# One decoder layer with GLA and DeltaNet heads on one core: the instruction order from the scheduler's timeline model in place of its default order

## The chip, the cores and the metric

The kernel runs on one core of one Trainium2 chip, as one program. The metric is the device time of one execution in microseconds; the kernel before takes 2975.47 us (median of three runs, 2974.47 to 2977.1).

## The reference, cut to what matters

One layer is computed for 512 prompt frames and 64 sample frames together, D = 2048, everything in float32:

```
mod = silu(c) @ w_ada + b_ada                   # 6 vectors of 2048, from 2048 x 12288 weights
h   = rmsnorm(x, norm1) * (1 + sc1) + sh1
proj = h @ w_in                                 # 2048 x 7200: 8 GDN heads, 4 GLA heads, gates
o_a = GLA(q, k, v, gate)                        # blocked causal recurrences
o_b = gated DeltaNet(conv(q), conv(k), conv(v)) # with a triangular solve per block
x  += g1 * (concat(o_a, o_b) @ w_out)
h   = rmsnorm(x, norm2) * (1 + sc2) + sh2
x  += g2 * (conv_ffn(h, w_up, w_down))          # 5632 wide, gate branch with a causal conv
y   = rmsnorm(x, final_norm)
```

The outputs are y for both streams and the new recurrent and convolution states.

## The kernel before, in words

The work is laid out with features on the 128 partitions and 576 frames on the free axis (two halves of 288). Each product is made in float32r parts: a weight tile of 128x1024 is loaded (`raw`), rounded by ACT into `wh` (L595) and DVE subtracts the rest, `wl` (L596); `mm6` (L508, L510) then issues three products (high by high, high by low, low by high), two matmuls each. This text calls these weight matmuls, and those of L774, L678, L679, L674 in the head and L1261 to L1263 in the FFN, gemm matmuls; the program has 18816 of them. A gemm tile of the input projection (`in_tile`) is 16 blocks of 128 rows of weights, 96 gemm matmuls.

The stages follow each other:

- The head (`head`): the first two blocks of the modulation are made on TensorE from `w_ada` (L674, and L678 and L679 with split weights), x is normalised and transposed, and the first two projection tiles run with it.
- The heads (`gdn_heads`, then `gla_heads`): for each of eight GDN heads four gemm tiles (q, k, v, gate), each followed by a convolution on ACT and DVE (`gdn_conv`, L880 to L891); then four GLA heads. Beside the gemms run *jobs*: Python generators (`gdn`, `gla`) that make the recurrence of a head, whose steps are emitted one per `tick`, after every mm6. A GDN job transposes k and q on PE (L140 in `transpose4`), makes decay tiles on ACT (`m<-m,ncum`, `m<-m,cum`, exponentials, `m<-m,nbeta`), solves a triangular system (`inverse16`: GpSimd for blocks of 16, with a trip through DRAM and L358 on DVE at its end, then levels L234, L240, L140, L249, L254 of PE and DVE in turn), and then goes through four blocks of 128 frames: L272 on PE, a correction on DVE (`sq`), L279 on PE, a copy on ACT (`sq`), L285 on PE, the new state on DVE (`st`), with L299 and L301 for the output, which ACT scales by `rq`. The rest ends with squares on ACT, L133 on DVE and L134 on GpSimd (an inverse root), four scalings `m<-m,s` and a transpose (L140). What a job issues on DVE and ACT goes through `_Sooner`, which lists it 80 places earlier in priority, and its record line is L1583.
- Also ticked: the rest of the modulation (`ada_blocks`, 16 blocks) is accumulated on DVE, from 512-KB loads of `w_ada` (`xr`): L736 first, then L738, two for each 128 rows of weights, and eight small matmuls (L744) at the end of a block.
- The output projection `w_out` with residual, then the FFN: 44 steps of seven products (`up_product`, L1261 to L1263), then `down`, then the final norm.

The buffers that the heads share are in `_MixPool`: 14 tiles `m`, 6 `qkv`, 3 `gt`. PSUM has two tiles `g` for gemm tiles and four `bank`s.

What sets the order: the kernel's Python code emits instructions in one sequence, with priorities (`high_priority`, offsets AHEAD and JOB_AHEAD), rests (`rest`, REST_T, REST_D, REST_X, REST_N: a job sits out so many steps) and rates (JOB_RATE, ADA_RATE). The tile layer's scheduler then lays this out as one in-order queue for each engine (PE, ACT, DVE, GpSimd as POOL, and SyncE as SP, which issues the DMAs), with semaphore waits where an instruction needs another engine's result. `TileContext` (L1641) is where the scheduler is chosen.

## Time and profile before

| | |
|---|---|
| median of three runs | 2975.47 us (2974.47 to 2977.1) |
| the profiled execution, its own time | 2976.19 us |
| span in its trace | 2974.5 us |
| TensorE's mean granted clock | 0.988 |
| busy: PE, DVE, ACT, POOL | 97%, 70%, 42%, 11% |
| read from and written to DRAM over the span | 131 GB/s |

One execution is recorded, and the times of the rows come from it. A window row gives the span of the window, then for PE, weight loads (PEld), DVE, ACT and POOL the busy time and in brackets the number of instructions, then the granted clock of TensorE as a share of full speed, the busy share of the DMA engines and GB/s. A row of waits gives the waiting engine and line, who released it, the total in us, how many times, and the longest. A group's row gives line, engine, operation, output and input tiles with their shapes and the count, then busy time in us, mean ns of one, then the idle time ahead of these instructions and what ended it. A timeline row gives start, duration, engine and line. float32 matmuls of the jobs run as two passes, each an entry of its own in the trace. L1583 stands for whatever a job issues on DVE and ACT.

### The profile page before, as it was taken

Reading aid. Unit: us, or ns where it says so; the run is one execution under the profiler, and the core shown is the slowest. Engines: PE = TensorE matmul, PEld = TensorE weight load, DVE = VectorE, ACT = ScalarE, POOL = GpSimd, SP = SyncE. Lnnn points to the kernel's source line nnn. Section 1 sums busy time; section 2 is a strip of 40 time slices with the busy share of each in tenths; the row PEclk is TensorE's granted clock in tenths of the full one; section 3 lists DMA queues with packets and bytes.
Section 4 is the critical chain, followed back from the end, with each engine's and each line's share of the span. In section 5 each row is a group of like instructions: output and inputs, shape, how many; then the busy total and the mean of one; then the engine's idle time right before and its main releaser. Section 6 shows DMA issues by size and latency. Waiting matters only on the chain.

```text
span 2974.5 us, 52619 instructions
## 1 busy us (share of the span) xinstructions
PE 2888.2 (97%) x21128; PEld 2786.8 (94%) x21128; DVE 2090.4 (70%) x3226; ACT 1238.0 (42%) x2116; POOL 340.5 (11%) x610
## 2 busy tenths in 40 slices
PE   7988999999999999999999999999999999999998
PEld 3588899999999998999999999999999999999997
DVE  5775667776578777357888888888888865555555
ACT  6555544544343333245444444444444431222223
POOL 0032333332200000000111111111101100000000
PEclk8999999999999999999999999999999999999999
DMA  7854545554444455543334333333333473333221
GB/s 270 290 143 135 148 125 148 146 149 139 138 141 142 137 164 160 158 142 94 105 105 116 105 105 109 112 98 106 115 105 105 135 235 102 111 102 116 83 83 66
DMA packets 532601, 392.96 MB, mean 132 GB/s; under 512 B 58729, under 2 KB 463204, under 8 KB 532356
## 3 DMA queue, kind: packets, MB, share of 16 engines
q1 hardware_dynamic: 532356, 389.59, 43.8%
q8 instruction: 167, 2.74, 0.4%
q14 instruction: 78, 0.64, 0.1%
HBM read 355.16 MB, written 34.36 MB: 131 GB/s over the span
## 4 chain that ended last, share of the span: by engine, by line
PE 65%; DVE 1%; DMA 1%; ACT 0%; issue 0%; POOL 0%; SPq 0%; ACTq 0%; POOLq 0%; DVEq 0%
PE g L508 20%; PE bank L1262 11%; PE bank L1261 11%; PE bank L1263 11%; PE g L510 10%; PE bank L401 1%; DVE acc L738 0%; PE bank L140 0%; DMA xr<-in_x_prompt_dram 0%; PE bank L744 0%; PE bank L1471 0%; POOL s L134 0%; DVE m L1583 0%; DMA raw<-in_w_out_dram 0%; DMA sd_ak<-ts 0%
## 5 line engine op out<-in xcount | busy, mean ns | idle before, releaser
L1262 PE MATMUL bank<-slot,wh 128*128 128x290 f32 x2464 | 736.7, 299 | 0.0
L1261 PE MATMUL bank<-slot,wh 128*128 128x290 f32 x2464 | 735.5, 298 | 0.0
L1263 PE MATMUL bank<-slot,wl 128*128 128x290 f32 x2464 | 728.0, 295 | 0.0
L508 PE MATMUL g<-slot,wh 128*128 128x288 f32 x3168 | 551.6, 295 | 0.2 <-DVE slot L1031 0.2
L595 ACT ACTIVATE wh<-raw 128x1024 fp32r<-128x1024 f32 x223 | 235.4, 1058 | 608.6 <-PE g L508 582.1
L1263 PEld LDWEIGHTS bank<-slot,wl 128*128 128x128 f32 x2464 | 471.8, 191 | 0.0
L1262 PEld LDWEIGHTS bank<-slot,wh 128*128 128x128 f32 x2464 | 469.5, 191 | 0.1
L508 PEld LDWEIGHTS g<-slot,wh 128*128 128x128 f32 x3168 | 465.1, 188 | 0.7 <-DVE slot L1031 0.5
L1261 PEld LDWEIGHTS bank<-slot,wh 128*128 128x128 f32 x2464 | 463.9, 188 | 0.1
L508 PE MATMUL g<-hh,wh 128*128 128x288 f32 x1984 | 453.1, 307 | 1.4 <-DVE cb L881 1.0
L510 PE MATMUL g<-hh,wl 128*128 128x288 f32 x1984 | 443.2, 302 | 3.2 <-DVE wl L596 3.2
L508 PE MATMUL g<-hl,wh 128*128 128x288 f32 x1984 | 439.8, 301 | 0.0
L1031 DVE SCALAR_TENSOR_TENSOR slot<-g,mod,slot 128x512 f32<-128x512 f32 (+1 forms) x448 | 201.8, 491 | 310.4 <-PE g L510 304.1
L738 DVE SCALAR_TENSOR_TENSOR acc<-xr,ct,acc 128x512 f32<-128x512 f32 x480 | 339.5, 753 | 37.0 <-DMA xr<-in_w_ada_dram 36.7
L510 PE MATMUL g<-slot,wl 128*128 128x288 f32 x1584 | 343.0, 295 | 0.0
L510 PEld LDWEIGHTS g<-hh,wl 128*128 128x128 f32 x1984 | 324.4, 191 | 4.2 <-DVE wl L596 3.7
L508 PEld LDWEIGHTS g<-hh,wh 128*128 128x128 f32 x1984 | 323.6, 191 | 4.9 <-DVE cb L881 1.2
L508 PEld LDWEIGHTS g<-hl,wh 128*128 128x128 f32 x1984 | 324.3, 191 | 1.1 <-issue 0.7
L596 DVE TENSOR_TENSOR wl<-raw,wh 128x1024 fp32r<-128x1024 f32 x223 | 272.2, 1222 | 55.2 <-ACT wh L595 54.5
L1208 ACT ACTIVATE wh<-raw 128x1024 fp32r<-128x1024 f32 x176 | 186.0, 1057 | 223.5 <-PE bank L1262 190.3
L510 PEld LDWEIGHTS g<-slot,wl 128*128 128x128 f32 x1584 | 255.1, 188 | 0.0
L1209 DVE TENSOR_TENSOR wl<-raw,wh 128x1024 fp32r<-128x1024 f32 x176 | 215.4, 1224 | 54.1 <-ACT wh L1208 54.1
(361 smaller groups left out, 3418.1 us busy)
## 6 DMA issues: line engine op xcount, KB each, us to landing
raw<-in_w_up_dram SPq DMA_DIRECT2D x176, 512.0 KB
xr<-in_w_ada_dram SPq DMA_DIRECT2D x128, 512.0 KB
raw<-in_w_in_dram SPq DMA_DIRECT2D x108, 512.0 KB
raw<-in_w_down_dram SPq DMA_DIRECT2D x88, 512.0 KB
hraw<-in_w_ada_dram SPq DMA_DIRECT2D x64, 512.0 KB
raw<-in_w_out_dram SPq DMA_DIRECT2D x32, 512.0 KB
slot<-actd SPq DMA_DIRECT2D x44, 288.0 KB
actd<-v SPq DMA_DIRECT2D x44, 256.0 KB
```

The source lines that it names most:

```text
L401: T.matmul(ps[:, b * 64:(b + 1) * 64], e3[:, b], qc[:, b * 64:(b + 1) * 64], start=True, stop=True)
L508: T.matmul(ps[:, h if bank is None else bank, :n], wh, x[:, h, :n], start=f, stop=False)
L510: T.matmul(ps[:, h if bank is None else bank, :n], wl, ah[:, h, :n], start=False, stop=stop)
L595: nc.scalar.activation(hi[:, :n_], raw[:, :n_], AF.Copy)
L596: nc.vector.tensor_tensor(lo[:, :n_], raw[:, :n_], hi[:, :n_].bitcast(F32), op=ALU.subtract)
L738: V.scalar_tensor_tensor(acc[s], w[:, k], col, acc[s], op0=ALU.mult, op1=ALU.add)
L1031: self.nc.vector.scalar_tensor_tensor(x1[:, :, z], ps[:, :, c], gain[:, q:q + 1], x1[:, :, z], op0=ALU.mult, op1=ALU.add)
L1208: self.nc.scalar.activation(hi, src, AF.Copy)
L1209: self.nc.vector.tensor_tensor(lo, src, hi.bitcast(F32), op=ALU.subtract)
L1261: T.matmul(ps, wh[:, j], hi, start=(c < 3 and j == 0), stop=False, skip_group_check=True)
L1262: T.matmul(ps, wh[:, j], lo, start=False, stop=False, skip_group_check=True)
L1263: T.matmul(ps, wl[:, j], hi, start=False, stop=(j == NPAIR - 1), skip_group_check=True)
```

## The change

One argument: the tile layer's scheduler is asked to place the instructions by a simulated timeline of the engines, in place of its default order.

```diff
-    with tile.TileContext(nc) as tc:
+    with tile.TileContext(nc, schedule_with_timeline_sim=True) as tc:
         layer_kernel(tc, i, o)
```

The instructions of both programs are the same, except that ACT loads its function tables five times more. What moves is the order on each engine, and with it the waits. The gemm matmuls keep their order among themselves in the heads. The steps of the GDN jobs stand later relative to them: counted in gemm matmuls on PE ahead of the same instruction, by 26 at the first (557 before, 583 now), 168 where 889 were, 837 where 1636 were, 875 where 2389 were; then the difference shrinks to 85 at 3659 and to about 30 at 5400. Some gemm tiles end with a stretch of job matmuls alone: 23 at gemm matmul 2496, 29 at 2880, 28 at 3264, 83 at 3552, 21 at 3648 and 80 at 3744; before, the longest in the heads is 20. SP issues the first loads of `w_in` 5 to 10 places earlier among those of `w_ada`. In the FFN the first two matmuls of the third and of the fifth of a step's products now stand ahead of the last 22 and 24 of the product before them.

Three places. The first is PE in an early GDN job, where a step of the inverse goes from L240 (`bank_420`) over DVE to the transpose L140 (`bank_421`). Before:

```order
L240 MATMUL bank_420_2279<-m_344_1674,m_384_2033 128x64 x4
L508 MATMUL g_471_2544<-hh_227_1048,wh_473_2546 128x288
L508 MATMUL g_471_2544<-hl_228_1049,wh_473_2546 128x288 x2
L510 MATMUL g_471_2544<-hh_227_1048,wl_474_2547 128x288 x2
L508 MATMUL g_471_2544<-hh_230_1071,wh_473_2546 128x288 x2
L508 MATMUL g_471_2544<-hl_231_1072,wh_473_2546 128x288
L140 MATMUL bank_421_2292<-consts0_91,m_385_2034 128x128 x4
L234 MATMUL bank_430_2329<-m_385_2034,m_359_1774 128x64 x4
```

Now, the last twelve rows ahead of and with the same transpose; its L240 stands seven rows above this piece:

```order
L508 MATMUL g_508_2895<-hh_167_828,wh_510_2897 128x288 x2
L508 MATMUL g_508_2895<-hl_168_829,wh_510_2897 128x288 x2
L510 MATMUL g_508_2895<-hh_167_828,wl_511_2898 128x288 x2
L508 MATMUL g_508_2895<-hh_170_851,wh_510_2897 128x288 x2
L508 MATMUL g_508_2895<-hl_171_852,wh_510_2897 128x288 x2
L510 MATMUL g_508_2895<-hh_170_851,wl_511_2898 128x288 x2
L508 MATMUL g_508_2895<-hh_227_1048,wh_510_2897 128x288 x2
L508 MATMUL g_508_2895<-hl_228_1049,wh_510_2897 128x288 x2
L510 MATMUL g_508_2895<-hh_227_1048,wl_511_2898 128x288 x2
L508 MATMUL g_508_2895<-hh_230_1071,wh_510_2897 128x288 x2
L508 MATMUL g_508_2895<-hl_231_1072,wh_510_2897 128x288
L140 MATMUL bank_421_2292<-consts0_91,m_385_2034 128x128 x4
```

Eight gemm matmuls stood between the two, and now 32 do.

The second is PE and ACT at the end of a GDN job, at gemm matmul 2880: from the last outputs (`bank_815`, `bank_822`, scaled by ACT into `m_791`) to the transpose of the normalised output (`bank_827`). PE before:

```order
L299 MATMUL bank_822_4990<-sq_819_4977,m_631_3736 128x128
L301 MATMUL bank_822_4990<-st_814_4952,qkv_605_3549 128x128
L510 MATMUL g_785_4828<-hh_322_1494,wl_812_4940 128x288 x2
L508 MATMUL g_830_5048<-hh_161_782,wh_832_5050 128x288 x2
L508 MATMUL g_830_5048<-hl_162_783,wh_832_5050 128x288 x2
L510 MATMUL g_830_5048<-hh_161_782,wl_833_5051 128x288 x2
L508 MATMUL g_830_5048<-hh_164_805,wh_832_5050 128x288 x2
L508 MATMUL g_830_5048<-hl_165_806,wh_832_5050 128x288 x2
```

PE now:

```order
L301 MATMUL bank_815_4954<-st_803_4908,qkv_605_3549 128x128
L272 MATMUL bank_816_4964<-st_814_4952,m_655_3930 128x128
L279 MATMUL bank_818_4975<-sq_817_4965,m_732_4427 128x128
L285 MATMUL bank_820_4986<-sq_819_4977,m_636_3768 128x128
L299 MATMUL bank_822_4990<-sq_819_4977,m_631_3736 128x128
L301 MATMUL bank_822_4990<-st_814_4952,qkv_605_3549 128x128
L140 MATMUL bank_827_5030<-consts0_91,m_791_4857 128x128
L744 MATMUL bank_850_5277<-consts0_91,acc_738_4530 128x1
```

The gemm matmuls of tile `g_830` followed the L301 of `bank_822`; now the transpose `bank_827` follows it at once. ACT there, before:

```order
L1583 ACTIVATE sq_825_5003,s8_823_5001<-m_791_4857 128x128
L595 ACTIVATE wh_845_5217<-raw_844_5216 128x1024
L1583 ACTIVATE m_791_4857<-bank_822_4990,rq_638_3780 128x128
L1583 ACTIVATE sq_825_5003,s8_823_5001<-m_791_4857 128x128
L930 ACTIVATE gt_828_5043<-g_785_4828 128x512
L1583 ACTIVATE sq_825_5003,s8_823_5001<-m_791_4857 128x128
L931 ACTIVATE ts_829_5045<-g_785_4828 128x64
L1583 ACTIVATE sq_825_5003,s8_823_5001<-m_791_4857 128x128
L1583 ACTIVATE m_791_4857<-m_791_4857,s8_824_5002 128x128 x4
```

ACT now, the last twelve rows of the same stretch; four scalings by ncum, an `sq`, a square, four scalings by cum and a table load stand between the scaling of `bank_815` and these rows:

```order
L1583 ACTIVATE m_867_5392<-m_867_5392 128x512
L1583 ACTIVATE sq_825_5003,s8_823_5001<-m_791_4857 128x128
L1583 ACTIVATE m_791_4857<-bank_822_4990,rq_638_3780 128x128
L890 ACT_TABLE_LOAD
L890 ACTIVATE qkv_975_6184<-ca_977_6186 128x512
L1583 ACT_TABLE_LOAD
L1583 ACTIVATE m_868_5393<-m_868_5393 128x512
L1583 ACTIVATE m_866_5390<-m_866_5390 128x512
L1583 ACTIVATE sq_825_5003,s8_823_5001<-m_791_4857 128x128
L1583 ACTIVATE m_867_5392<-m_867_5392,nbeta_1609 128x128 x4
L886 ACTIVATE ca_1018_6464<-cb_1017_6463,cols_172 128x579
L1583 ACTIVATE sq_825_5003,s8_823_5001<-m_791_4857 128x128
```

Between the scaling of `bank_815` and the four scalings `m_791<-m_791,s8_824`, which come next now, the opening of the next head's job (tiles `m_866` to `m_868`, with `L890` and `L886` of a convolution and three table loads) has moved in.

The third is DVE at gemm matmul 3552, in the next job's inverse: from the masking of `bank_1112` to that of `bank_1116` (`m_984`), with the update of `m_1087` between. Before:

```order
L1583 TENSOR_TENSOR m_984_6216<-bank_1112_7108,consts384_1530 128x256
L133 TENSOR_SCALAR s8_1105_7063<-s8_1104_7062 128x4
L738 SCALAR_TENSOR_TENSOR acc_1069_6756<-xr_1143_7326,ct_186,acc_1069_6756 128x512
L738 SCALAR_TENSOR_TENSOR acc_1070_6757<-xr_1143_7326,ct_186,acc_1070_6757 128x512
L1583 TENSOR_TENSOR m_1087_6911<-m_1087_6911,bank_1113_7121 128x16x16
L133 TENSOR_SCALAR rq_1110_7089<-s8_1109_7088 128x4
L1583 TENSOR_SCALAR rq_1110_7089<-rq_1110_7089 128x4
L1583 TENSOR_TENSOR m_984_6216<-bank_1116_7148,consts384_1530 128x256
L1583 TENSOR_TENSOR m_1087_6911<-m_1087_6911,bank_1117_7161 128x8x32
L1583 COPY m_984_6216<-bank_1122_7192 64x256
L1583 COPY m_1087_6911<-bank_1123_7205 64x4x64
```

Now:

```order
L1583 TENSOR_TENSOR m_984_6216<-bank_1112_7108,consts384_1530 128x256
L738 SCALAR_TENSOR_TENSOR acc_1069_6756<-xr_1084_6896,ct_186,acc_1069_6756 128x512
L738 SCALAR_TENSOR_TENSOR acc_1070_6757<-xr_1084_6896,ct_186,acc_1070_6757 128x512
L133 TENSOR_SCALAR rq_1110_7089<-s8_1109_7088 128x4
L738 SCALAR_TENSOR_TENSOR acc_1069_6756<-xr_1084_6896,ct_186,acc_1069_6756 128x512
L738 SCALAR_TENSOR_TENSOR acc_1070_6757<-xr_1084_6896,ct_186,acc_1070_6757 128x512
L1583 TENSOR_TENSOR m_1087_6911<-m_1087_6911,bank_1113_7121 128x16x16
L738 SCALAR_TENSOR_TENSOR acc_1069_6756<-xr_1088_6947,ct_186,acc_1069_6756 128x512
L1583 TENSOR_SCALAR rq_1110_7089<-rq_1110_7089 128x4
L738 SCALAR_TENSOR_TENSOR acc_1070_6757<-xr_1088_6947,ct_186,acc_1070_6757 128x512
L738 SCALAR_TENSOR_TENSOR acc_1069_6756<-xr_1088_6947,ct_186,acc_1069_6756 128x512
L738 SCALAR_TENSOR_TENSOR acc_1070_6757<-xr_1088_6947,ct_186,acc_1070_6757 128x512
```

Before, the L738 for the modulation stood ahead of the chain's steps and two of them inside it; now they stand between each step and the next.

## The prediction

> **What bounds the kernel now.** I read the page first, then the windows, then PE's waits by stretch, then the groups by line on ACT and DVE. The page's first part and the first row of its slices:
>
> ```profile
> span 2974.5 us, 52619 instructions
> ...
> PE 2888.2 (97%) x21128; PEld 2786.8 (94%) x21128; DVE 2090.4 (70%) x3226; ACT 1238.0 (42%) x2116; POOL 340.5 (11%) x610
> ...
> PE   7988999999999999999999999999999999999998
> ```
>
> PE is the bound: busy 97% of the span. The profiled execution took 2976.19 us, 0.7 us over the median of the three timed runs (2975.47); I sum against 2976.2. What the change can win lies in the 86.3 us in which PE was not busy and in time at a lower clock. Where that is, the windows show (columns: span, PE busy, PEld, DVE, ACT, POOL, granted clock, DMA share, GB/s):
>
> ```profile
> 0.00:200.00 200.00, 173.76 (x908) 116.33 (x908) 137.40 (x247) 123.75 (x216) 14.12 (x32) 0.95 0.77 251
> 200.00:300.00 100.00, 87.52 (x635) 85.26 (x635) 63.77 (x100) 49.55 (x124) 41.03 (x85) 0.91 0.44 124
> 300.00:400.00 100.00, 94.67 (x713) 91.17 (x711) 68.54 (x115) 45.93 (x123) 32.58 (x59) 0.97 0.49 139
> 400.00:600.00 200.00, 190.40 (x1423) 184.29 (x1424) 136.98 (x222) 98.19 (x254) 68.13 (x131) 0.97 0.51 145
> 600.00:800.00 200.00, 194.08 (x1475) 185.97 (x1474) 130.58 (x216) 94.13 (x236) 57.06 (x121) 1.00 0.48 137
> 800.00:1000.00 200.00, 195.08 (x1434) 185.50 (x1434) 149.99 (x277) 79.93 (x145) 4.59 (x5) 0.99 0.51 148
> 1000.00:1400.00 400.00, 391.21 (x2873) 379.08 (x2872) 256.09 (x462) 158.04 (x292) 13.60 (x41) 0.99 0.50 143
> 1400.00:2900.00 1500.00, 1500.00 (x11215) 1499.99 (x11213) 1104.21 (x1478) 565.61 (x668) 105.89 (x131) 1.00 0.37 112
> ```
>
> From 1400 to 2900 us (the FFN) PE never stops, so nothing is to be won there. The head (0 to 200) leaves 26.2 us idle. Between 200 and 600, the first four or so GDN heads, 27.4 us are idle (12.5 + 5.3 + 9.6), and the mean clocks 0.91, 0.97 and 0.97 take another 9 + 3 + 6 = 18 us of PE's pace. From 600 to 1400 it is 19.6 us idle (5.9 + 4.9 + 8.8).
>
> Who is waited for there: PE's waits from 150 to 300, then from 300 to 500 (total, times, longest):
>
> ```profile
> PE bank L140 <- ACT m L1583: 11.9, 3, 9.5
> PE g L510 <- DVE wl L596: 3.2, 1, 3.2
> ```
>
> ```profile
> PE bank L140 <- ACT m L1583: 10.3, 3, 4.8
> PE bank L140 <- ACT qkv L890: 2.2, 1, 2.2
> ```
>
> So 24.4 us of the early idle time are transposes (L140) of a GDN job that stand in PE's queue ahead of gemm matmuls and wait for ACT, a few gemm rows after the step they depend on. The longest, in the timeline:
>
> ```profile
> 227.66 1.29 DVE L358 TENSOR_TENSOR m<-cm,consts 128x512 f32<-128x512 f32 x2 [7.97 <-DMA cm<-d]
> ...
> 229.06 0.28 ACT L1583 ACTIVATE sq<-bank 128x128 f32<-128x128 f32 x1 [9.42 <-DVE s L133]
> ...
> 240.28 0.48 PE L140 MATMUL bank<-consts,m 128*128 128x128 f32 x1 [9.53 <-ACT m L1583]
> ```
>
> DVE stood 8 us behind L358, which waits for inverse16's DMA; L133 queued behind it, so ACT stood 9.4 us, and PE 9.5 us later. These chains are sensitive to what stands in a queue between two steps.
>
> **The change part by part.** The instructions are the same but for five more ACT table loads; only the order moves.
>
> *Early heads (gain).* In before 3 to 10 gemm matmuls stand between dependent steps of a job; now some 23 do, about 3 us of PE work, while a step on DVE or ACT is well under 1 us. The job steps fall ever further behind the gemms: at gemm matmul 1057 by 168, at 2473 by 837, at 3264 by 875. I take all 24.4 us of L140's early waits as gone, and a third of the 18 us of clock, 6 us, as these waits are the longest idle stretches there. The rest (L510 for DVE, issue) stays. Ends: 20 (one of the long waits returns) to 45 (all 27.4 and all 18). Later waits, 500 to 1400:
>
> ```profile
> PE bank L240 <- DVE m L1583: 3.4, 3, 1.2
> PE bank L140 <- ACT m L1583: 3.2, 7, 0.9
> ...
> PE bank L140 <- ACT qkv L890: 2.2, 2, 1.8
> PE bank L140 <- DVE m L1583: 0.6, 1, 0.6
> ```
>
> These 9.4 us are GDN hops of the same kind; I take them as gone, since what the late GDN steps cost now is counted whole below.
>
> *Plateaus (loss).* A job that is behind keeps its m, qkv and gt buffers, and the gemm tile that needs one is held. So in the new order gemm tiles (96 matmuls each) are separated by stretches in which only job matmuls stand on PE: 23 at gemm matmul 2496, 29 at 2880, 28 at 3264, 83 at 3552, 80 at 3744; before, no such stretch in the heads is over 20. There the chain's own ACT and DVE work is uncovered. At 2880 the transpose of bank_827 waits for ACT, whose queue now holds, from the scaling of bank_815 on, a whole opening of the next head. Its prices (busy us and mean ns of one; I divide busy by count):
>
> ```profile
> L1583 ACT ACTIVATE m<-m 128x512 f32<-128x512 f32 x63 | 37.2, 624 | 21.9 <-DVE m L1583 21.5
> ...
> L1583 ACT ACT_TABLE_LOAD x16 | 20.5, 1283 | 0.3
> L886 ACT ACTIVATE ca<-cb,cols 128x579 f32<-128x579 f32 x24 | 18.6, 776 | 12.2 <-DVE cb L881 12.2
> ...
> L890 ACT ACTIVATE qkv<-ca 128x512 f32<-128x512 f32 x24 | 15.1, 630 | 38.9 <-DVE ca L888 38.7
> ...
> L1583 ACT ACTIVATE m<-bank,rq 128x128 f32<-128x128 f32 x36 | 13.1, 364 | 25.4 <-PE bank L301 20.3 <-PE bank L297 5.1
> ...
> L1583 ACT ACTIVATE m<-m,ncum 128x128 f32<-128x128 f32 x36 | 12.4, 391 | 27.3 <-DMA m<-gd 27.3
> ...
> L1583 ACT ACTIVATE m<-m,nbeta 128x128 f32<-128x128 f32 x36 | 11.6, 389 | 2.6 <-POOL m L175 2.5
> ...
> L1583 ACT ACTIVATE m<-m,s 128x128 f32<-128x128 f32 x36 | 11.5, 391 | 19.7 <-POOL s L134 19.6
> ...
> L1583 ACT ACTIVATE sq<-m 128x128 f32<-128x128 f32 x36 | 11.1, 309 | 0.6
> ...
> L1583 ACT ACTIVATION_READ_ACCUMULATOR sq<-m 128x1 f32 x36 | 6.8, 190 | 0.0
> ```
>
> Eight scalings by ncum and cum at 0.34 = 2.8; four squares with their read at 0.31 + 0.19 = 2.0; three 128x512 at 0.59 = 1.8; three table loads at 1.28 = 3.8; L890 0.63, L886 0.78; four by nbeta 1.3 and four by s 1.3; two rq scalings 0.73 and an sq 0.3: 15.4 us. Beside it PE has five job matmuls, each in two passes of 0.115 us by the timeline row below (16 passes in 1.84 us), so 1.2 us, and a wait for the first of them. Loss about 13 us. The same count at 3264 gives 15.4 against 2.2, another 13; at 2496, 14.9 against 7.9, 7.
>
> ```profile
> 569.03 1.84 PE L744 MATMUL bank<-consts,acc 128*128 128x1 f32 x16
> ```
>
> At 3552 the bottleneck is DVE. Its rows:
>
> ```profile
> L738 DVE SCALAR_TENSOR_TENSOR acc<-xr,ct,acc 128x512 f32<-128x512 f32 x480 | 339.5, 753 | 37.0 <-DMA xr<-in_w_ada_dram 36.7
> L596 DVE TENSOR_TENSOR wl<-raw,wh 128x1024 fp32r<-128x1024 f32 x223 | 272.2, 1222 | 55.2 <-ACT wh L595 54.5 <-PE bank L377 0.2
> ...
> L358 DVE TENSOR_TENSOR m<-cm,consts 128x512 f32<-128x512 f32 x18 | 12.0, 688 | 19.8 <-DMA cm<-d 19.7
> ```
>
> Between the first step of the plateau and the L234 at 3850 stand 172 DVE instructions, 90 of them L738, which used to stand beside gemm matmuls. Two to five of them now stand between one job step and the next. At 753 ns 90 take 68 us (at 0.71, their busy time by count, 64); with six L596 (7.5), six L736 and the 70 job instructions the queue holds 100 to 108 us. PE has 298 gemm matmuls at 1500 us / 11215 = 0.134 (the FFN's window), 40 us, and some 180 job instructions at 0.23, 41 us: 81 us together. Loss 19 to 27; as PE's and DVE's rows also wait for each other, step by step, I take 30 (up to 45). Two L358 stand in the chain here, and the inverse they wait for is issued later than before: 5 us by its row's 19.7 in 4 waits (0 to 8).
>
> *Clock.* The 15 us around the long wait, and the 22 after it:
>
> ```profile
> 225.00:240.00 15.00, 5.76 (x44) 5.52 (x42) 4.17 (x9) 8.61 (x26) 4.22 (x7) 0.83 0.54 161
> 240.00:262.00 22.00, 21.72 (x162) 20.82 (x162) 8.46 (x14) 10.98 (x25) 8.54 (x30) 0.88 0.33 89
> ```
>
> After an idle stretch of 9.5 us PE works on at a lower clock: 0.88 over 22 us is 2.6 us lost. Five plateaus with such idle stretches: 8 us, up to 20 if the two long ones stay at half speed while their job matmuls run. [...]
>
> The extra table loads are inside the counts above (3 x 1.28 us). [...]
>
> *Head, FFN, tail.* SP issues the first w_in loads 5 to 10 places sooner, ahead of w_ada loads. The head is fed by DMA at 251 GB/s; some 1 MB moved is 4 us either way, and I take 0. In the FFN two matmuls of one weight product move ahead of the last 22 or 24 of the one before it. PE is at 1500.00 of 1500 there, so I take 0; if their split came just too late each time, 43 tiles by one 1.22-us subtraction would be 52 us.
>
> **The sum:** 7 + 13 + 13 + 30 + 5 + 8 = +76; less 24.4 + 6 + 9.4 = 39.8: +36, so 3012 us, as the profiled execution counts; on the median's scale 3011.5, and I write 3012.
>
> **The rivals.** *Faster or no change.* The new spacing wins the whole of the pool between 200 and 1400 us: 27.4 + 19.6 idle and 18 + 6 of clock (0.99 over 600 us) = 71 us, and the plateaus cost only their queue sums by busy time, 7 + 13 + 13 + 19 = 52: 2957 us. It decides where the plateaus stay under 71 us. For it: every dependent step up to gemm matmul 2400 gets 3 us of cover. Against it: half of the pool lies in short pieces that no order of these steps touches (GLA, DMA of x, issue), and queue sums leave out latencies. If only the early 45 and the later 9.4 go, the same plateaus give 52 - 54.4, no change: 2974.
>
> *Much slower.* In the plateau at 3552, L738 also waits for its own loads (its row has 36.7 us for xr's DMA): 90 of them use a 512-KB tile each 3 us, twice over for the w_in tiles beside; three waits of 8 us add 24, and half clock throughout the two long plateaus 12 more: 3048. The row against it: DMA's share is only 0.48 to 0.51 there.
>
> *The FFN's swap costs,* up to 52 us: 3064 us. Against it: the full 1500 us.
>
> **How the numbers follow.** About 0.2% (6 us) is what a measurement of this kernel can tell from no change. Forecast +36: 0.68. Faster or none: 0.09 faster (2957), 0.09 within 0.2% (2974). Much slower 0.11, FFN 0.03. So slower is 0.82. The range takes the forecast's ends: low, 52 and 8 of clock against 45 + 9.4, 2981; high, 7 + 13 + 13 + 45 + 8 + 20 = 106 against the early 30 alone, 3052.
>
> **What would show it.** Right: L140's waits before 450 us nearly gone and the clock there 0.97 or more; PE's largest waits between 500 and 780 us, L140 for ACT (about 13 us twice) and, near 680 to 730 us, L240, L140 and L254 for DVE with L738 as DVE's busiest line; PE busy 100% from 1430 on. Wrong: gemm waits in the FFN; a head longer by over 5 us; or plateaus in which PE waits under 40 us in all.

## The result, and the profile after

The changed kernel takes 3075.72 us (median of four runs, 3071.37 to 3081.13) against 2975.18 for the kernel before: ratio 1.0338, 95% interval 1.0319 to 1.0356. It is slower, as forecast, but by 100 us where 36 were forecast, and above the range of 2981 to 3052. One of the four executions of e2 below took 5079 us at a mean granted clock of 0.76, and it was the recorded one, so e2's ratio goes by the other three and e5 repeats its kernel for a trace. The page of the changed kernel:

```profile
span 3075.9 us, 52646 instructions
...
PE 2922.6 (95%) x21128; PEld 2829.3 (92%) x21128; DVE 2086.2 (68%) x3226; ACT 1246.9 (41%) x2121; POOL 291.0 (9%) x610
...
PE   7999998888779999999999999999999999999998
...
PEclk8999998898769999899999999999999999999999
```

The span grew by 101.4 us. PE's busy time grew by 34.4 (2888.2 to 2922.6) for the same matmuls, at a mean granted clock of 0.961 in place of 0.988, and its idle time by 67 (86.3 to 153.3). The slices where PE's digit and its clock fell, the seventh to the twelfth, are 461 to 923 us. The windows of the prediction, after:

```profile
0.00:200.00 200.00, 171.75 (x889) 115.97 (x890) 132.65 (x239) 114.70 (x192) 14.17 (x32) 0.94 0.76 245
200.00:300.00 100.00, 95.13 (x723) 93.73 (x722) 52.67 (x81) 50.47 (x114) 35.28 (x87) 0.98 0.41 116
300.00:400.00 100.00, 94.65 (x731) 93.95 (x730) 67.02 (x105) 41.94 (x101) 28.30 (x51) 0.98 0.49 143
400.00:600.00 200.00, 181.58 (x1347) 179.22 (x1346) 110.37 (x176) 87.96 (x215) 49.72 (x102) 0.93 0.43 124
600.00:800.00 200.00, 159.27 (x1098) 153.66 (x1099) 114.45 (x192) 81.68 (x227) 39.81 (x92) 0.82 0.41 118
800.00:1000.00 200.00, 172.00 (x1160) 162.02 (x1160) 119.50 (x219) 70.09 (x175) 29.41 (x67) 0.84 0.43 123
1000.00:1400.00 400.00, 390.06 (x2801) 375.22 (x2801) 270.40 (x495) 148.46 (x265) 9.33 (x26) 0.97 0.53 153
```

From 200 to 300 us PE is now busy 95 us at 0.98, where it was 87.5 at 0.91. From 600 to 1000 it is idle 69 us, where it was 11, and the clock is 0.82 and 0.84. PE's waits after, 150 to 300 us, 500 to 800 and 800 to 1100:

```profile
PE bank L140 <- ACT m L1583: 4.2, 2, 3.5
```

```profile
PE bank L140 <- ACT m L1583: 38.1, 4, 12.2
PE bank L240 <- DVE m L1583: 3.7, 2, 2.0
PE bank L285 <- ACT sq L1583: 3.7, 6, 1.0
```

```profile
PE g L508 <- ACT ts L1010: 8.6, 2, 6.9
PE bank L240 <- DVE m L1583: 4.2, 1, 4.2
PE bank L285 <- ACT sq L1583: 4.2, 6, 1.9
```

The early wait of 11.9 us for ACT is down to 4.2; four waits of the same kind, 38 us, have come at the ends of the gemm tiles that the order pointed at. Since the gemm matmuls keep their order, both traces can be read at the same gemm matmul (counted in the trace; us from the span's start):

| gemm matmul | before | after | change in this piece | other than gemm matmuls in this piece, before, after |
|---|---|---|---|---|
| 480 | 163.3 | 170.5 | +7.2 | 119, 125 |
| 2400 | 556.3 | 498.5 | -65.0 | 457, 270 |
| 3400 | 739.6 | 721.5 | +39.7 | 210, 221 |
| 3850 | 831.3 | 913.5 | +100.3 | 128, 246 |
| 5660 | 1165.0 | 1246.6 | -0.6 | 336, 374 |
| 6000 | 1223.2 | 1321.5 | +16.7 | 48, 62 |
| 18800 | 2956.7 | 3060.1 | +5.1 | |

At gemm matmul 2400 the changed kernel is 58 us ahead, but 181 of the others (job matmuls, the modulation's L744) have not been done yet; at 0.23 us each (two passes; 16 passes of L744 took 1.84 us before the change), and half of that for the 56 transposes among them, which have one entry each in the trace (four of L140 are four below, four of L240 are eight), that is by this estimate some 35 us of PE work that it owes, and some 23 us are really won. Between 3400 and 3850 it pays: 118 more job matmuls than before (50 of them transposes), 21 us of work by the same count, take 100 us.

The piece from gemm matmul 3551, where the first of the long stretches begins, to 3850, which the prediction priced:

```profile
746.85:913.50 166.65, 118.45 (x662) 107.64 (x660) 96.83 (x173) 62.70 (x185) 38.76 (x88) 0.69 0.41 118
```

It takes 166.7 us. DVE is busy 96.8 of them. PE is busy 118.5, at a mean clock of 0.69, for work that the prediction counted as 81 us at full clock, so by this estimate some 37 us are lower clock; and it is idle 48 us.

What a payment looks like: the windows of the stretches at gemm matmuls 2880 and 3264 (their later part, with the long wait), 3552 and 3744.

```profile
596.00:613.00 17.00, 6.92 (x33) 6.92 (x34) 6.35 (x13) 12.85 (x32) 3.76 (x7) 0.50 0.03 7
684.00:699.00 15.00, 6.16 (x29) 6.16 (x30) 5.58 (x11) 10.85 (x28) 3.17 (x6) 0.50 0.02 4
747.00:797.00 50.00, 29.80 (x147) 25.99 (x146) 30.84 (x56) 20.59 (x69) 10.52 (x20) 0.62 0.43 126
843.00:897.00 54.00, 31.55 (x139) 25.96 (x138) 32.75 (x59) 17.78 (x48) 4.68 (x11) 0.57 0.39 118
```

In none of them is any engine full from end to end: DVE, the one I had named for the last two, is busy 62% and 61%, PE 60% and 58% at little over half clock. In the stretch at 3552 the limit changes from part to part. From 747 to 755 us the block loop runs at a granted clock of 1.00, with PE, DVE and ACT in turn; then PE waits 7.8 us for ACT (L140); then come the levels of the inverse at half clock (0.50 from 764 to 795 us). The timeline of PE from 772 us shows two of these levels; ahead of it stand four rows of DVE between two of its steps:

```profile
774.62 1.41 DVE L738 SCALAR_TENSOR_TENSOR acc<-xr,ct,acc 128x512 f32<-128x512 f32 x2
775.94 0.41 DVE L1583 TENSOR_TENSOR m<-m,bank 128x256 f32<-128x256 f32 x1
776.27 0.75 DVE L738 SCALAR_TENSOR_TENSOR acc<-xr,ct,acc 128x512 f32<-128x512 f32 x1
...
779.64 0.75 DVE L738 SCALAR_TENSOR_TENSOR acc<-xr,ct,acc 128x512 f32<-128x512 f32 x1 [0.56 <-DMA xr<-in_w_ada_dram]
```

```profile
772.59 1.94 PE L240 MATMUL bank<-m,m 128*128 128x64 f32 x8 [1.95 <-DVE m L1583]
776.41 1.12 PE L140 MATMUL bank<-consts,m 128*128 128x128 f32 x4 [1.88 <-DVE m L1583]
777.32 1.81 PE L234 MATMUL bank<-m,m 128*128 128x64 f32 x8
780.87 1.94 PE L240 MATMUL bank<-m,m 128*128 128x64 f32 x8 [1.75 <-DVE m L1583]
783.91 1.12 PE L140 MATMUL bank<-consts,m 128*128 128x128 f32 x4 [1.10 <-DVE m L1583]
```

L240 ends, DVE first works off two L738, then takes the step, then PE transposes: the engines take turns, and the eight passes of L234 or L240 take 1.8 to 1.9 us where before the change they took 1.0 to 1.1. One level, from one L140 to the next (12 job matmuls, four of them transposes):

```profile
776.41:783.91 7.50, 4.66 (x20) 4.31 (x21) 6.88 (x13) 0.38 (x1) 0.00 (x0) 0.50 0.47 143
```

It takes 7.50 us, with PE busy 4.66 at half clock and DVE busy 6.88; in this part DVE, with L738, is nearly full.

### The profile page after: what moved, and what is told of

It is laid out like the page before. It is cut to its first block, busy times and chain, and to the rows that moved or that the text cites. A ratio compares the mean times of both kernels' runs of the same rounds, so it can differ in the third digit from the quotient of the medians.

```text
span 3075.9 us, 52646 instructions
## 1 busy us (share of the span) xinstructions
PE 2922.6 (95%) x21128; PEld 2829.3 (92%) x21128; DVE 2086.2 (68%) x3226; ACT 1246.9 (41%) x2121; POOL 291.0 (9%) x610
## 4 chain that ended last, share of the span: by engine, by line
PE 68%; DVE 2%; DMA 2%; ACT 1%; issue 0%; POOL 0%; SPq 0%; ACTq 0%; DVEq 0%; POOLq 0%
PE g L508 21%; PE bank L1262 11%; PE g L510 11%; PE bank L1261 11%; PE bank L1263 11%; DVE acc L738 1%; PE bank L401 1%; DMA xr<-in_w_ada_dram 1%; PE bank L744 1%; PE bank L140 1%; PE bank L1471 0%; DMA xr<-in_x_prompt_dram 0%; PE bank L443 0%; PE bank L437 0%; DMA raw<-in_w_out_dram 0%
## 5 line engine op out<-in xcount | busy, mean ns | idle before, releaser
L1263 PE MATMUL bank<-slot,wl 128*128 128x290 f32 x2464 | 715.9, 296 | 1.1 <-DVE wl L1209 1.1
L508 PE MATMUL g<-hh,wh 128*128 128x288 f32 x1984 | 445.4, 304 | 12.8 <-ACT ts L1010 8.6
L738 DVE SCALAR_TENSOR_TENSOR acc<-xr,ct,acc 128x512 f32<-128x512 f32 x480 | 338.6, 750 | 33.6 <-DMA xr<-in_w_ada_dram 33.1
```

What stands on the lines that cost most here:

```text
L508: T.matmul(ps[:, h if bank is None else bank, :n], wh, x[:, h, :n], start=f, stop=False)
L738: V.scalar_tensor_tensor(acc[s], w[:, k], col, acc[s], op0=ALU.mult, op1=ALU.add)
L1263: T.matmul(ps, wl[:, j], hi, start=False, stop=(j == NPAIR - 1), skip_group_check=True)
```

## The experiments

Each kernel was timed beside the kernel before on the same chip, whose median was 2979 to 2984 us there; so ratios are compared, and 0.001 is 3 us. The changed kernel's is 1.0338 (1.0319 to 1.0356). e5 and e12 were executed once each and serve for their traces alone.

Theory A, formed after the traces: in the new order two dependent steps of a GDN job's levels and block loop stand a median of 26 gemm matmuls apart, nine in ten of them 23 or more (pairs up to gemm matmul 2490; before, a median of 5), so the chain of a job runs slower than the gemms, and its steps are owed; owed steps are paid later without cover, with the engines taking turns and PE at half clock. The price is 0.60 us per job matmul at 3552 (50 us for 83) and 0.68 at 3744 (54 for 80), where among gemm matmuls one takes 0.23 (a transpose half of that). Theory B, my forecast's: DVE, filled with L738 between the steps, sets the length of the two long stretches. Theory C: gemm tiles are held for a buffer, and that is the loss.

**e1: two more qkv buffers.**

```diff
-    BUFS = {"m": 14, "qkv": 6, "gt": 3}
+    BUFS = {"m": 14, "qkv": 8, "gt": 3}
```

> The changed order with eight qkv buffers in place of six. In this order the stretches of job matmuls at gemm matmuls 2496, 2880 and 3264 go, and what was owed is stacked at 3456 (34), 3552 (46) and 3744 (148); the number of job matmuls still owed when tile 3744 begins is the same. Theory A (debt: each dependent step of a job stands at least 23 gemm matmuls behind the one before it, so the jobs fall behind, and what is owed is paid later as a bare chain, wherever buffers let it stand): within 15 us of the changed kernel, 3060 to 3090. Theory C (the loss is made by gemm tiles that are held for a buffer): the three early stretches cost about 33 us, so 3030 to 3050.

Ratio 1.0253 (1.0237 to 1.0268), 25 us below the changed kernel, between the two. In its trace gemm matmul 3400 comes at 665.6 us in place of 721.5, and the one long stretch at 3744 takes this window:

```profile
784.00:875.00 91.00, 56.37 (x255) 47.38 (x254) 57.70 (x109) 36.41 (x115) 19.21 (x48) 0.59 0.45 124
```

So the holds at 2496, 2880 and 3264 cost something by themselves, as C has it; but of the 56 us that this kernel is ahead at 3400, with 56 fewer of the other matmuls done, it gives back 34 by 3850, where as many are done, in stretches at the same price: 148 job matmuls in 91 us, 0.61 each. Buffers decide where the debt is paid, and a part of how much.

**e2, e5 and e3: without most of the modulation.** e2 and e5 are the changed order, e3 the default order, each with only the first two of 16 steps of every later modulation block.

```diff
-        for k0 in range(0, KD, 2):
+        for k0 in range(0, 2, 2):
```

> The changed order with 14 of 16 steps of every later modulation block left out (no L738 but two of every thirty, their loads too), so the outputs that use the modulation are not the layer's. Theory B (my forecast's: DVE, filled with L738 between the job's steps, sets the length of the long stretches at 3552 and 3744): these shrink from 54 and 58 us to 25 or less, and the kernel is less than 40 us above its partner e3 (the default order with the same left out). Theory A (the chain from engine to engine sets it, with PE at half clock): still 70 and 64 job matmuls there, each stretch over 35 us, and 60 us or more above e3.

> The default order (the kernel before) with the same 14 of 16 steps of every later modulation block left out. Partner of e2. Both theories: PE sets the time here, so 2955 to 2976; it is the base from which e2 is counted.

> The kernel of e2 again, for an undisturbed profile: the changed order with 14 of 16 steps of the later modulation blocks left out (outputs that use it are not the layer's). The question is the price of one job matmul in the long stretches (70 at gemm matmul 3552, 64 at 3744), which in the changed kernel and in e1 is 0.60 to 0.68 us each (50 us for 83, 54 for 80, 91 for 148). Theory A (bare chain, PE at half clock): 0.5 us or more, 35 us and 32 us or longer. Theory B (DVE's L738 between the steps): 0.35 or less, under 25 us each.

e2 came to 1.0097 (1.0078 to 1.0116), e3 to 1.0035 (1.0020 to 1.0049): 18 us apart, under the 40 that B forecast for the whole, where A had 60 or more. The stretches say otherwise. Their windows in e5:

```profile
726.70:766.80 40.10, 25.55 (x121) 21.96 (x120) 9.61 (x21) 19.63 (x67) 4.31 (x5) 0.57 0.15 44
813.20:849.70 36.50, 25.01 (x112) 19.75 (x112) 9.44 (x21) 14.57 (x45) 1.28 (x3) 0.63 0.17 47
```

With DVE busy only 24% and 26%, 70 job matmuls still take 40 us and 64 take 36.5: 0.57 each, where B asked for 0.35 or less. The level shown above takes, in e5:

```profile
749.33:755.11 5.78, 4.66 (x20) 4.31 (x20) 0.85 (x2) 0.38 (x1) 0.00 (x0) 0.50 0.13 45
```

So 1.7 us of the 7.50 go with L738; PE alone, at half clock, is 4.66 of the 5.78 that are left. Over the whole stretches L738 makes 0.03 to 0.11 of 0.60 to 0.68, and in the second a part of that is no job step: 6.9 of its 54 us are the next gemm matmul waiting for ACT (`ts`, L1010), against 2.8 in e5. Taking turns at half clock is most of the price. The whole comes out closer for other reasons. The default order without the modulation is itself slower than the kernel before, which neither theory had: it comes to gemm matmul 2400 27 us later (583.5 against 556.3), but has done 88 more of the other matmuls by then (664 against 576), up to 20 us of work; at 5660, where as many are done (1258 and 1250), it is 21 us later, and why stays open. Fewer steps are owed in the changed one (134 in the two long stretches in place of 163). And it has no late loads of the modulation (e10, below).

**e4 and e9: filling the gaps.** Extra 128x128 matmuls into the bank that the next step is about to overwrite, so that PE does not idle between two steps of the last heads: two ahead of each step in e4, four in e9.

```diff
-        return self.pm.tile([P, 512], F32, tag="bank", name=self.name("bank"))
+        return self.warmed(warm, self.pm.tile([P, 512], F32, tag="bank", name=self.name("bank")))
...
+def _warmed(self, warm, ps):
+    for _ in range(4 if warm else 0):
+        self.nc.tensor.matmul(ps[:, :P], self.c["ident"], self.c["ident"], start=True, stop=True)
+    return ps
```

> The changed order with two extra 128x128 matmuls (result not used) ahead of each step of the inverse's levels and of the block loop in the last three GDN heads: 126 more, 74 of them in the long stretches. If half the loss in the long stretches is PE's clock (theory A's second half): granted clock there above 0.85 in place of 0.61 to 0.65, the stretches 10 us or more shorter each, and 5 to 20 us below the changed kernel although 52 of the extra matmuls (0.23 us each, 12 us) stand among gemm matmuls. If the clock there costs nothing because the chain waits for DVE and ACT anyway: 10 to 30 us above the changed kernel.

> The changed order with four extra 128x128 matmuls (result not used) ahead of each step of the levels of the sixth and seventh heads' jobs (counted from 0) and of the block loop of the fifth to seventh from its second block: 192 more, 50 in the stretch at 3552, 64 in that at 3744, 57 among gemm matmuls (13 us). In e4, two of them left the clock at 0.64 in the first stretch and brought 0.78 in the second. If the clock is what makes a bare step dear: 0.85 or more in both, and the stretches 45 us or shorter, though PE has 12 and 15 us more to do in them. If the clock comes back and the stretches are 55 us or longer: the steps' latency on DVE and ACT is the price and full speed wins nothing there. If the clock stays under 0.75: open.

e4: 1.0359 (1.0343 to 1.0376), 6 us above the changed kernel, with intervals that overlap. e9: 1.0377 (1.0361 to 1.0392), 12 us above. The two stretches in e4, then in e9:

```profile
759.00:807.00 48.00, 34.02 (x182) 31.55 (x182) 29.88 (x54) 19.83 (x67) 5.18 (x5) 0.64 0.40 114
853.00:903.00 50.00, 34.06 (x223) 29.85 (x222) 33.09 (x60) 17.89 (x49) 4.96 (x13) 0.78 0.45 131
```

```profile
757.80:805.60 47.80, 32.78 (x246) 31.10 (x245) 27.76 (x52) 19.87 (x68) 6.05 (x8) 0.86 0.38 107
859.30:917.60 58.30, 40.80 (x267) 37.18 (x267) 31.45 (x58) 17.85 (x48) 3.98 (x11) 0.77 0.38 111
```

In e9's first stretch the clock is back at 0.86 and the length hardly moves, 47.8 us for 50.0 with 50 extra matmuls (12 us) in it; the second, at 0.77, is 4 us longer with 64 extra. Neither of the clean outcomes. The same level in e9, with eight extra matmuls in it:

```profile
790.01:796.77 6.76, 4.38 (x36) 4.08 (x37) 6.16 (x12) 0.39 (x1) 0.00 (x0) 1.00 0.54 158
```

At a clock of 1.00 in place of 0.50 the level is 0.7 us shorter, and DVE with its L738 is busy 6.16 of 6.76: where the clock is back, as here, DVE's queue takes its place. What this leaves open is whether the clock counts when DVE is not in the way.

**e12: both.** The kernel of e5 with the extra matmuls of e9.

> The kernel of e5 (the changed order, 14 of 16 steps of the later modulation blocks left out, so outputs that use it are not the layer's) with the four extra matmuls of e9: 27 of them in the stretch at 3552 (97 in place of 70), up to 56 in that at 3744 (120 in place of 64). Neither L738 nor half clock is left to lengthen a step. In e5 the stretches took 40 and 36 us. If the clock is a part of a bare step's price that e9 did not show because DVE took its place: granted clock 0.85 or more and 35 us or less in the first. If PE, DVE and ACT taking turns is the price: 38 us or more in the first at any clock.

```profile
737.80:771.00 33.20, 22.17 (x174) 20.52 (x173) 7.61 (x17) 18.92 (x65) 4.32 (x5) 0.90 0.16 50
822.50:862.50 40.00, 30.53 (x224) 27.81 (x223) 10.04 (x22) 16.57 (x47) 4.58 (x14) 0.86 0.15 43
```

The first stretch falls from 40.1 to 33.2 us though 27 matmuls more stand in it, with the clock at 0.90 in place of 0.57: so the clock is a part of the price, 7 us or more of that stretch. The second holds 56 extra matmuls (13 us of PE) and is 3.5 us longer. In the first, PE is still idle a third of the time with little L738 and nearly full clock; that rest is taking turns, the longest wait 5.7 us (L140 for ACT). The level, again with eight extra matmuls in it:

```profile
757.55:762.21 4.66, 4.15 (x36) 4.01 (x36) 0.84 (x2) 0.38 (x1) 0.00 (x0) 1.00 0.16 56
```

So it takes 7.50 us with L738 and half clock, 6.76 without half clock, 5.78 without L738 and 4.66 without either, where its twelve matmuls among gemm matmuls would take some 2.3 (eight at 0.23, four at half of that).

**e10 and e11: the modulation sooner.** The last two loads of the modulation fall late in the changed kernel, among those for x and w_up; SP's timeline, and the window around it, after, and then the piece before the change:

```profile
1265.00 0.38 SPq L730 DMA_DIRECT2D xr<-in_w_ada_dram  x1
...
1274.67 1.16 SPq L1202 DMA_DIRECT2D raw<-in_w_up_dram  x2
1275.93 1.62 SPq L730 DMA_DIRECT2D xr<-in_w_ada_dram  x1
```

```profile
1246.00:1322.00 76.00, 68.65 (x431) 61.30 (x430) 30.99 (x50) 21.09 (x38) 1.11 (x5) 0.87 0.65 179
```

```profile
1165.00:1224.00 59.00, 55.57 (x404) 52.63 (x403) 25.81 (x38) 17.16 (x30) 0.24 (x3) 1.00 0.81 217
```

e10 raises ADA_RATE, e11 has e1's buffers as well.

```diff
-JOB_RATE, ADA_RATE = 1.0, 0.65
+JOB_RATE, ADA_RATE = 1.0, 0.85
```

> The changed order with ADA_RATE 0.85 in place of 0.65: the modulation is done by gemm matmul 4800 in place of 5800, with 120 L738 in place of 90 between gemm matmuls 3551 and 3850. If the late modulation is what the changed kernel loses between 5660 and 6000 (its last w_ada loads at 1265 and 1276 us, beside those of x and w_up; 74.9 us against 58.2): that piece 62 us or shorter. If L738 between the job's steps sets the long stretches (theory B): 3400 to 3850 longer by 20 us or more than the changed kernel's 192, and the kernel not faster. Under theory A it is longer by 10 at most, and the whole 3055 to 3070.

> The changed order with both: eight qkv buffers (25 us in e1) and ADA_RATE 0.85. If the two act apart, the gain is the sum of those of e1 and e10: 3030 to 3045. If the extra L738 lengthen the one long stretch at 3744 (156 job matmuls): 3055 or more.

e10: 1.0471 (1.0456 to 1.0487), 40 us above the changed kernel; e11: 1.0408 (1.0390 to 1.0425). The piece from 5660 to 6000 went as expected, from 74.9 to 52.3 us, PE full and at full clock:

```profile
1313.00:1365.50 52.50, 52.50 (x388) 50.63 (x386) 16.60 (x25) 13.87 (x26) 0.72 (x7) 1.00 0.72 187
```

But the rest went the other way: 3400 to 3850 takes 211.5 us in place of 192, almost the 20 that I had set for B; the piece at 2400 to 2496, 44 in place of 27; 4032 to 4800, 169 in place of 146. My limits for theory A, 10 us and a faster kernel, fell. Yet the 20 us do not stand where B puts them: the two long stretches take 104 us for 171 job matmuls, 0.61 each, where the changed kernel takes 102 for 163, and the level shown above takes 7.64 us in place of 7.50, with DVE as busy (6.87 us). The rest is 10 us between them and 7 behind the second. In the first of these places PE waits 7.3 us (L279) for a DVE step that stands behind an L358, which waits 5.1 us for its DMA; in the second it waits 5.5 us for another L358 (L234). Inside the first long stretch the modulation's own L744 waits 6.0 us for L738. So the higher rate costs time around the job steps, but e10 does not show that more L738 make a bare step dearer. e11 against e10 gains 19 us, where e1 gained 25, so the buffers gain much the same with either rate.

**e6, e7, e8: does a little more distance help the default order?** If cover between dependent steps is worth the 23 us won early, the default order with somewhat more of it should win some.

```diff
-JOB_RATE, ADA_RATE = 1.0, 0.65
+JOB_RATE, ADA_RATE = 0.8, 0.65
```

In e7 it is 0.7; e8 keeps 1.0 and puts half of `REST_X` ahead of the two L358:

```diff
-        t, u = self.m4(), self.m4()
+        t, u, _ = self.m4(), self.m4(), (yield from self.rest(REST_X // 2))
...
-        yield from self.rest(REST_X)
+        yield from self.rest(REST_X - REST_X // 2)
```

> The default order with JOB_RATE 0.8 in place of 1.0: dependent job steps stand 6 to 8 gemm matmuls apart in place of 2 to 6, and at most 15 job matmuls are owed at gemm matmul 2400. If cover between dependent steps is what the changed kernel wins early (theory A): the L140 waits before 500 us (24 us) fall by a third or more, 2960 to 2970. If the early gain came from something else (the head, the clock): 2972 to 2980.

> The default order with JOB_RATE 0.7: steps 6 to 12 gemm matmuls apart, 54 job matmuls owed at gemm matmul 2400 and at 3552, and no stretch of 17 or more of them alone. Theory A: owing costs nothing as long as nothing is paid bare, so the early waits fall by half or more and nothing is given back: 2950 to 2966. If being behind costs by itself (buffers held longer): 2980 to 3000.

> The default order with the two L358 issued half of REST_X (8 job steps) later, which moves them some 50 to 95 gemm matmuls later on DVE in the first heads. If DVE standing behind L358's wait for DMA (19.7 us in four waits) is what makes the 9.5-us wait of PE at 230 us: L358's waits under 8 us in all, the 9.5-us wait gone, 2962 to 2970. If that chain waits for something else anyway (the gd load, the table load): 2972 to 2978.

All three are a little slower than the kernel before: 1.0047 (1.0030 to 1.0064), 1.0054 (1.0038 to 1.0070), 1.0025 (1.0015 to 1.0035). The transposes' waits for ACT fall in e6 and e7 (8.1 and 5.1 us, where 22.2 were), as theory A had it, but others came in their place; PE's largest from 150 to 500 us in e6, e7 and e8:

```profile
PE bank L272 <- DVE st L1583: 19.9, 3, 8.3
PE bank L140 <- ACT m L1583: 8.1, 9, 2.0
```

```profile
PE bank L240 <- DVE m L1583: 15.3, 2, 8.7
PE bank L140 <- ACT qkv L890: 8.3, 1, 8.3
```

```profile
PE bank L140 <- ACT m L1583: 24.9, 5, 10.7
```

Six to twelve gemm matmuls (0.8 to 1.6 us) do not cover a wait of 8 to 10 us, and L358's own waits fell from 19.7 to 11.7 us in e8 without PE's falling. So these runs do not bear out that a moderately wider spacing wins; that the changed kernel wins its 23 us by cover is read from its waits alone. None of the kernels tried beats the kernel before.

## Why the prediction was wrong

The direction, the places and the mechanism by which gemm tiles end in bare job steps were right. What failed is the step that priced the long stretches by their fullest queue, and with it the size of the clock's term.

- *The long stretches* ("Loss 19 to 27; ... I take 30 (up to 45)", with 5 for L358): between 3400 and 3850 the changed kernel lost 100.3 us, of them 21 for 118 more job matmuls: 79 in place of 35. I had added up each engine's queue and taken the fullest, DVE with 100 to 108 us. That queue was read rightly, DVE is busy 96.8 us there; but the piece takes 166.7. A chain in which PE, DVE and ACT wait for each other, each the limit in another part, takes longer than the queue that is fullest over the whole. That DVE's queue is not the greater part e5 shows, with DVE three quarters idle: 0.57 us per job matmul, against 0.60 and 0.68. A sum hop by hop would have had to add each matmul to its DVE or ACT step; I have done it for one level only.
- *The clock* ("8 us, up to 20 if the two long ones stay at half speed"): in the piece from 3551 to 3850 PE is busy 118.5 us for 81 of work, some 37 us of lower clock; over the whole program its busy time grew by 34.4 net. No run shows the 8 us; five times the 2.6 us of the trace before would be 13. I had given each stretch one dip after it; in the trace the clock stays at half through most of the stretch (0.62 and 0.57 in the mean). The 37 us are not all loss: in e9 a clock of 0.86 hardly shortened the first stretch, in e12, without L738, it took 7 us or more off it.
- *The short stretches* (7 + 13 + 13 us): from 2400 to 3400 the loss is 39.7, 37 after the 11 more job matmuls; with the clock's share in it the terms hold. The waits stood where the prediction put them, 11.9 us at 2880 and 12.2 at 3264.
- *The early heads* (24.4 + 6): the lead at 2400 is 65 us over that piece, but 187 job matmuls fewer are in it, some 37 us: 28 really won there, 23 after the head. The waits went as said; most of the lead was a loan.
- *Late GDN waits* (-9.4): 3850 to 5660 is 0.6 us faster with 38 more job matmuls (up to 9 us): right.
- *Head, w_out, FFN* (0 each): +7 in the head, over the 5 that the prediction had set as a sign of being wrong; +16.7 from 5660 to 6000, where the last loads of the modulation, due late, stand among those of x and w_up (e10 took it away; PE's waits there are 7.4 us in all, the rest is a clock of 0.87 and 14 more job matmuls), a term that was not in my list; +5 at the start of the FFN (gemm matmuls 7000 to 7500) and nothing from there on, so the swap in the FFN costs next to nothing: its gemm waits are 1.1 and 0.6 us.

Of the rivals, "much slower" was nearest (3048), for half of its reason: half clock through the long stretches, 8 + 12 us there and some 37 in the trace. The other half, L738 waiting for its own loads, was small: these waits are 7.8 us from 747 to 897 us, where the rival had 24, and 33 over the whole kernel, 37 before.

Not settled: how the 0.60 to 0.68 us divide over a whole stretch. For one level the four runs above divide it; the block loop and the ends of the jobs were not taken apart in the same way.

## What to carry to other kernels

An order that puts more independent work between dependent steps looks like a gain for as long as the delayed chain may lag; read the lead only after subtracting the work that is still owed, and look for the place where it falls due. Where steps stand on an in-order queue with no cover, price them as a chain, hop by hop at the clock that such a stretch gets (0.62 and 0.57 here), not by the queue that is fullest over the whole of it. A scheduler's own timeline had no advantage over a default order that was spaced by hand here.

## What the runs showed of the hardware

In the stretch at 3552 the clock stays at half without any long idle stretch. It falls in the 7.8-us wait of L140 for ACT that ends at 762.9 us (1.00 from 747 to 758 us, 0.52 from 758 to 764). From 764 to 795 us the longest wait of PE is 1.95 us, PE is busy 71% of the time, and the granted clock is 0.50; in the first 6.5 us of it PE's records leave no idle time at all:

```profile
764.00:795.00 31.00, 21.90 (x104) 20.06 (x103) 25.55 (x45) 10.73 (x36) 4.33 (x4) 0.50 0.49 147
764.10:770.60 6.50, 6.50 (x31) 6.35 (x31) 4.40 (x8) 5.60 (x17) 1.44 (x2) 0.50 0.23 58
```

In e12's stretches, with PE busy 67% and 76%, it was 0.90 and 0.86, so busy share alone, which half clock itself raises (eight passes of L234 take 1.81 us at 0.50, and 1.00 at 1.00 before the change), does not tell the two apart. Before the change the clock was 0.50 behind the 9.5-us wait that ends at 240.3 us, and 1.00 again from 246 us on:

```profile
240.28:245.00 4.72, 4.72 (x21) 4.72 (x22) 0.00 (x0) 4.60 (x11) 0.00 (x0) 0.50 0.00 0
246.00:262.00 16.00, 16.00 (x136) 15.10 (x134) 8.40 (x14) 5.10 (x13) 8.54 (x30) 1.00 0.45 122
```

There it was back after less than 6 us without a gap in PE's records; in the changed kernel 6.5 us without one did not bring it back, and no run shows what was lacking.
